# Float32r products with stacked split parts for the samples' A, the decay gates, and the diagonal and last level of a GLA head

## The chip, the cores and the metric

One core of one Trainium2 chip runs the whole program. The metric is the device time of one execution in microseconds; the time of a version is the median of its runs.

## The reference

One layer of a hybrid decoder runs on 256 prompt tokens and on 8 samples of 8 tokens (320 tokens, model width 2048), in float32:

```python
h = rmsnorm(x);  proj = h @ w_in          # q, k, v, gates of both branches
log_a = log_sigmoid(gal @ gla_alpha_up + gla_alpha_bias) / 16      # gal: 16 wide
# GLA head, chunk of L tokens (128 prompt, 8 sample); b = cumsum(log_a)
a_mat[t, s] = sum_d q[t, d] k[s, d] exp(b[t, d] - b[s, d])   for s <= t
o = a_mat @ v + (q * exp(b)) @ S
# mLSTM head: the same with one decay per token, D, and a normaliser column
num = (q k^T * D) @ v + w_inter * (q @ C);  den = the same on a column of ones
x = x + (sig(g_A) * (y_m @ W_A) + sig(g_B) * (y_g @ W_B)) @ W_out
x = x + ConvFFN(rmsnorm(x))
```

There are 4 heads of each branch (GLA: 128 keys, 256 values; mLSTM: 256 and 256). The outputs are y and the new states.

## The kernel before, in words

Activations lie transposed: features on the partitions, 320 tokens in the free dimension. Every large product is done in float32r on split operands: `weights` (L63) loads 512 KB, ScalarE rounds it (L69, `wh`), VectorE takes the rest (L70, `wl`), and `mm3` (L73) multiplies high by high (L74), high by low (L75) and low by high (L76), each a 128x128 weight against 320 columns. Weights pass through rings of 3 (`wh`, `wl`) and 4 (`raw`) buffers; products land in 4 PSUM banks named `big`, everything else in 4 named `mx`.

The work in order: norm and first projections (to 48 us), the gate block L310 to L408, then for each of 4 heads the projection of v, `gla_head` (L551), the projections of q, k and v, and `mlstm_head` (L654), to about 480 us; then gates, branch and output products and the ConvFFN, to the end. The program is given to a scheduler that runs a timeline simulation and writes one fixed order for each engine's queue. Engines keep that order, so an instruction that waits holds back everything behind it on its engine. In the head stage the scheduler mixes the small products of a head with the large products of the next projections on TensorE.

What the change touches:

- **Decay gates.** L297 loads the 16x512 matrix `alup` by a POOL DMA to partitions 64 to 79. L330 evacuates `galT`. L346 makes four float32 products of 16 rows, 320 columns each.
- **`values`** (L449), run once per head of each branch: v is transposed, ScalarE and VectorE write `vH` and `vL` (L463, L464), `vt` is a float32 copy for the samples (L468), `vs` holds v of 32 sample tokens four times over, the lower two quarters reduced to the low part (L470, L471). POOL writes the columns of ones and zeros on each call (L461, L462, L466).
- **`gla_head`**: the matrix A^T (`AT`) is filled by parts. L563 makes its diagonal: three float32 products k^T q, of 128, 128 and 64 tokens, from which only the diagonal is taken (L564, L565). L566 runs over eight levels hh = 128, 64, ..., 1: VectorE forms the decay exponents (L577, L578), ScalarE the exponential (L579), POOL multiplies k and q by it (L580, L581), and TensorE multiplies in float32 (L589 for each half of the prompt, L598 for the samples where hh <= 4), and VectorE copies the level's blocks by a mask (L592, L600).
- **Samples' A times v.** `inter` (L535) sums q times the old state into `pi`; then POOL (L609, in GLA) or VectorE (L708, in mLSTM) spreads the 64x64 sample A over `asp`, and one float32 product of 64 rows adds it to `pi` (L610, L710). `numerators` (L474) does the prompt's part on split operands (L485).
- **State updates** L645 and L732 multiply `vs` by masked keys in float32r.
- L408 and L669 pass the mLSTM gate rows through DRAM and back, spread over the partitions (`bc`), on POOL's DMA queue; L680 is the first reader.

A float32 matrix product shows in the trace as two records for each call, a float32r product or a transpose as one.

Of the kernel before, what the change touches and what calls it, by code (L numbers as in the profile page):

```python
# [17 lines left out]
P = 128  # L18
# [4 lines left out]
S = 8  # L23
# [20 lines left out]
def step_kernel(ctx: ExitStack, tc: tile.TileContext, a: dict):  # L44
# [52 lines left out]
    ones = cp.tile([P, P], F32, name="ones")  # L97
    nc.vector.memset(ones, 1.0)
    epsc = cp.tile([P, 1], F32, name="epsc")
    nc.gpsimd.memset(epsc, EPS)  # L100
# [132 lines left out]
    with tc.tile_pool(name="mc", bufs=1, reuse_waits="tile") as mc, \  # L233
# [61 lines left out]

        alup = mg.tile([P, 512], F32, name="alup")
        nc.gpsimd.dma_start(alup[64:80], a["gla_alpha_up"][0])  # L297
        mp9 = mc.tile([4, 9], F32, name="mp9")
# [30 lines left out]
        galT = mg.tile([P, N], F32, name="galT")  # L329
        nc.vector.tensor_tensor(galT[64:80], pg[64:80, :N], rstd_bc[64:80], op=ALU.mult)  # L330
        fr = w320("fr")[32:36]
        nc.vector.tensor_tensor(fr, pg[32:36, :N], rstd_bc[32:36], op=ALU.mult)
# [11 lines left out]
        for h in range(H):  # L344
            pz = mx("mx10")
            nc.tensor.matmul(pz[:, :N], alup[64:80, h * P:(h + 1) * P], galT[64:80], start=True, stop=True)  # L346
            xb = w320("xb")
            nc.vector.tensor_scalar(xb, pz[:, :N], abias[:, h:h + 1], None, op0=ALU.add)
            gb.append(gb5[:, h])
            nc.vector.scalar_tensor_tensor(gb[h], xb, -1.0, xb, op0=ALU.mult, op1=ALU.min)  # L350
            gx.append(xb)
# [60 lines left out]

        asp = mc.tile([64, P], F32, name="asp")
        nc.gpsimd.memset(asp, 0.0)

# [33 lines left out]
        def values(v):  # L449

            pb = mx("mx8")
            for m in range(2):
                vr, vr4 = quads("vr")
                nc.gpsimd.tensor_copy(vr4, tok4(v[:, m, T:]))
                for g in range(2):
                    nc.tensor.transpose(pb[:, g * 256 + m * P:g * 256 + (m + 1) * P], vr[:, g * P:(g + 1) * P], ident)
            pa = natural(v)
            pav = pa.rearrange("p (j e) -> p j e", j=2)
            vH = wk.tile([P, 2, 264], F32R, tag="vH", name="vH", bufs=1)[:, :, 0:258]
            vL = wk.tile([P, 2, 264], F32R, tag="vL", name="vL", bufs=1)[:, :, 0:258]  # L460
            nc.gpsimd.memset(vH[:, :, 256:258].bitcast(F32), 1.0)  # L461
            nc.gpsimd.memset(vL[:, :, 256:258].bitcast(F32), 0.0)  # L462
            nc.scalar.activation(vH[:, :, 0:256], pav, AF.Copy)  # L463
            nc.vector.tensor_tensor(vL[:, :, 0:256], pav, vH[:, :, 0:256].bitcast(F32), op=ALU.subtract)  # L464
            vt = wk.tile([64, 260], F32, tag="vt", name="vt", bufs=1)
            nc.gpsimd.memset(vt[:, 256:257], 1.0)  # L466
            for g in range(2):
                nc.scalar.copy(vt[32 * g:32 * g + 32, 0:256], pb[32 * g:32 * g + 32, g * 256:(g + 1) * 256])  # L468
            vs = wk.tile([P, 512], F32R, tag="vs", name="vs", bufs=1)
            nc.scalar.activation(vs, pb, AF.Copy)  # L470
            nc.vector.tensor_tensor(vs[64:128], pb[64:128], vs[64:128].bitcast(F32), op=ALU.subtract)  # L471
            return (vH, vL, vt), vs

        def numerators(name, A, vn, w):  # L474

            vH, vL, vt = vn
            AH = wk.tile([P, 384], F32R, tag="AH", name="AH", bufs=1)
# [73 lines left out]
        def gla_head(h, q, k, v):  # L551

            st0 = wk.tile([P, B, DV + 4], F32, tag="state", name="S0", bufs=3)[:, :, 0:DV]
            nc.sync.dma_start(st0, a["state_gla_S"][0, :, h].rearrange("b d e -> d b e"))
            vn, vs = values(v)
            b = gb[h]
            AT = wk.tile([P, 512], F32, tag="AT", name="AT")
            nc.gpsimd.memset(AT, 0.0)
            ATp = AT.rearrange("p (j c) -> p j c", j=2)[:, :, 0:P]
            ATs = AT[0:64, 384:448]  # L560
            pd = mx("mx11")
            for j, (t0, tn) in enumerate(TOK):
                nc.tensor.matmul(pd[:tn, t0:t0 + tn], k[:, t0:t0 + tn], q[:, t0:t0 + tn], start=True, stop=True)  # L563
            nc.vector.copy_predicated(ATp, dg8, pd[:, 0:256].rearrange("p (j c) -> p j c", j=2))  # L564
            nc.vector.copy_predicated(ATs, dg8[0:64, 0, 0:64], pd[0:64, 256:320])  # L565
            for hh in (128, 64, 32, 16, 8, 4, 2, 1):  # L566
                w = N if hh <= 4 else T
# [40 lines left out]
            pi = inter(qe, lambda b, d: st0[:, b], 256)  # L608
            nc.gpsimd.tensor_copy(srows(asp), ATs.rearrange("p (g q t) -> p g q t", g=2, q=4))  # L609
            nc.tensor.matmul(pi[:, 0:256], asp, vn[2][:, 0:256], start=False, stop=True)  # L610
            normed(list(numerators("mx13", AT, vn, 256)) + [pi], ghw[:, 2 * h:2 * h + 2], 8 + 2 * h)
# [25 lines left out]
            for b0 in range(0, B, 4):  # L637
# [4 lines left out]
                for i in range(0, 4, 2):  # L642
                    pS = mx("mx16")
                    for ii in range(2):
                        nc.tensor.matmul(pS[:, ii * 256:(ii + 1) * 256], kmv[:, i + ii], vs[:, 64 * b0:64 * b0 + 256],  # L645
                                         start=True, stop=True)
                    for ii in range(2):
                        bb = b0 + i + ii
                        nc.vector.scalar_tensor_tensor(st0[:, bb], st0[:, bb], ebe[:, bb:bb + 1],
                                                       pS[:, ii * 256:(ii + 1) * 256], op0=ALU.mult, op1=ALU.add)  # L650
# [3 lines left out]
        def mlstm_head(h, q, k, v):  # L654
            c0t = []
            for half in range(2):
# [3 lines left out]
                c0t.append(t)  # L660
            vn, vs = values(v)
            pa = natural(k)
# [22 lines left out]
            for half in range(2):  # L685
                nc.gpsimd.tensor_copy(c0t[half][:, :, :, DH], n0h[:, :, 4 * half:4 * half + 4].rearrange("p d b -> p b d"))
            n1 = nT[:, :, 4:36].rearrange("p d (b h) -> p d b h", h=H)[:, :, :, h]
# [12 lines left out]
            ks = stacked(pk, 512)  # L700
            pi = inter(qi, lambda b, d: c0t[b // 4][:, b % 4, d, 0:DH + 1], DH + 1)
            pS = mx("mx18")
            for d in range(2):
# [3 lines left out]
            nc.vector.tensor_tensor(D[:, 0:384], D[:, 0:384], pS[:, 0:384], op=ALU.mult)  # L707
            nc.vector.tensor_tensor(srows(asp), D[0:64, 384:448].rearrange("p (g q t) -> p g q t", g=2, q=4),  # L708
                                    pS[0:64, 384:448].rearrange("p (g q t) -> p g q t", g=2, q=4), op=ALU.mult)
            nc.tensor.matmul(pi[:, 0:DH + 1], asp, vn[2][:, 0:DH + 1], start=False, stop=True)  # L710
            normed(list(numerators("mx21", D, vn, DH + 2)) + [pi], mhw[:, 2 * h:2 * h + 2], 2 * h,
# [10 lines left out]
            for b0 in range(0, B, 2):  # L722
# [5 lines left out]
                for i in range(2):  # L728
                    bb = b0 + i
                    pC = mx("mx24")  # L730
                    for d in range(2):
                        nc.tensor.matmul(pC[:, d * 256:(d + 1) * 256], kmv[:, i, d * P:(d + 1) * P],  # L732
                                         vs[:, 256 * (b0 // 4):256 * (b0 // 4) + 256], start=True, stop=True)
                    cf = c0t[bb // 4][:, bb % 4, :, 0:DH]
# [246 lines left out]
```

## Time and profile before

| | us |
|---|---|
| median of 3 runs (1931.51 to 1933.71) | 1931.62 |
| the profiled execution, its own time | 1933.11 |
| its span, first to last instruction | 1931.4 |
| TensorE busy in the span | 1914.0 |
| VectorE / ScalarE / GpSimd busy | 1069.6 / 763.1 / 325.6 |

The span is 1.7 us below the execution's own time, and that execution is 1.5 us above the median. Busy time of TensorE counts a matmul until its result has left the array, so neighbours overlap in it; what one costs is read from the distance of the starts.

### The profile page before, as it was taken

The numbers are of one execution on the slowest core, as the hardware profiler recorded it, in microseconds if no ns is written. First come the engines' busy times: TensorE is split into PE (matmuls) and PEld (weight loads), VectorE is DVE, ScalarE is ACT, GpSimd is POOL, SyncE is SP. The second block draws the span as 40 slices with busy tenths as digits, with TensorE's granted clock in tenths as the row PEclk, the third lists the DMA queues.
The fourth block names the chain that finished last, engine by engine and source line by source line (L and its number), as shares of the span: only waits on it lengthen the run. The fifth ranks groups of instructions, "written<-read, shape, count | busy, mean of one in ns | idle before, by whom it ended". The sixth has DMA issues, their size and how long they took to land.

```text
span 1931.4 us, 32475 instructions
## 1 busy us (share of the span) xinstructions
PE 1914.0 (99%) x13143; PEld 1886.9 (98%) x13143; DVE 1069.6 (55%) x1627; ACT 763.1 (40%) x1063; POOL 325.6 (17%) x622
## 2 busy tenths in 40 slices
PE   9999999999999999999999999999999999999997
PEld 8989999999999999999999999999999999999997
DVE  5757676767544444445555545545554554555455
ACT  5434343454433333333344333433433343333335
POOL 4222232333000000012121101201110120111014
PEclk9999999999999999999999999999999999999999
DMA  8646666666655555556444444444444444444442
GB/s 238 197 117 191 196 186 202 189 194 191 193 148 148 152 153 146 149 156 202 146 149 152 153 147 149 153 151 144 152 153 148 148 153 152 144 152 153 149 148 95
DMA packets 300128, 310.96 MB, mean 161 GB/s; under 512 B 15237, under 2 KB 291995, under 8 KB 299978
## 3 DMA queue, kind: packets, MB, share of 16 engines
q1 hardware_dynamic: 287849, 283.53, 48.7%
q0 software_dynamic: 7232, 23.84, 3.6%
q8 instruction: 103, 1.69, 0.4%
q10 hardware_dynamic: 4896, 1.52, 0.3%
q14 instruction: 48, 0.39, 0.1%
HBM read 286.37 MB, written 22.47 MB: 160 GB/s over the span
## 4 chain that ended last, share of the span: by engine, by line


## 5 line engine op out<-in xcount | busy, mean ns | idle before, releaser
L70 DVE TENSOR_TENSOR wl<-raw,wh 128x1024 fp32r<-128x1024 f32 x504 | 629.2, 1248 | 623.9 <-ACT wh L69 623.0
L69 ACT ACTIVATE wh<-raw 128x1024 fp32r<-128x1024 f32 x504 | 534.3, 1060 | 900.0 <-PE big L75 766.2
L74 PE MATMUL big<-hH,wh 128*128 128x320 f32 x2832 | 880.6, 311 | 0.0
L75 PE MATMUL big<-hL,wh 128*128 128x320 f32 x2832 | 880.3, 311 | 0.0
L76 PE MATMUL big<-hH,wl 128*128 128x320 f32 x2832 | 879.6, 311 | 0.0
L76 PEld LDWEIGHTS big<-hH,wl 128*128 128x128 f32 x2832 | 533.1, 188 | 3.2 <-issue 2.6
L74 PEld LDWEIGHTS big<-hH,wh 128*128 128x128 f32 x2832 | 533.5, 188 | 1.9 <-issue 1.2
L75 PEld LDWEIGHTS big<-hL,wh 128*128 128x128 f32 x2832 | 533.4, 188 | 0.9 <-issue 0.4
L75 PE MATMUL big<-aL,wh 128*128 128x320 f32 x704 | 217.9, 310 | 0.0
L76 PE MATMUL big<-aH,wl 128*128 128x320 f32 x704 | 217.6, 309 | 0.0
L74 PE MATMUL big<-aH,wh 128*128 128x320 f32 x704 | 215.8, 309 | 0.0
L76 PEld LDWEIGHTS big<-aH,wl 128*128 128x128 f32 x704 | 132.4, 188 | 0.0
L75 PEld LDWEIGHTS big<-aL,wh 128*128 128x128 f32 x704 | 132.4, 188 | 0.0
L74 PEld LDWEIGHTS big<-aH,wh 128*128 128x128 f32 x704 | 131.8, 188 | 0.0
L876 POOL COPY conv<-u 128x2 f32<-128x2 f32 x44 | 8.2, 186 | 527.5 <-DVE u L873 527.5
L75 PE MATMUL big<-mL,wh 128*128 128x320 f32 x256 | 78.8, 309 | 0.0
L74 PE MATMUL big<-mH,wh 128*128 128x320 f32 x256 | 78.7, 309 | 0.0
L76 PE MATMUL big<-mH,wl 128*128 128x320 f32 x256 | 78.7, 309 | 0.0
L807 POOL TENSOR_TENSOR g<-g 128x320 f32<-128x320 f32 x16 | 14.7, 919 | 369.6 <-DVE g L803 369.6
L914 DVE TENSOR_TENSOR x<-big,x 128x320 f32<-128x320 f32 x96 | 46.6, 488 | 44.4 <-PE big L76 44.3
L888 POOL TENSOR_TENSOR g<-g,uc 128x256 f32<-128x256 f32 x44 | 32.5, 739 | 211.9 <-DVE g L887 211.9
L75 PE MATMUL big<-yL,wh 128*128 128x320 f32 x192 | 59.2, 308 | 0.0
(360 smaller groups left out, 1751.0 us busy)
## 6 DMA issues: line engine op xcount, KB each, us to landing
raw<-in_w_in SPq DMA_DIRECT2D x176, 512.0 KB, 3.7
raw<-in_ffn_w_up SPq DMA_DIRECT2D x88, 512.0 KB, 3.5
raw<-in_ffn_w_gate SPq DMA_DIRECT2D x88, 512.0 KB, 3.5
raw<-in_ffn_w_down SPq DMA_DIRECT2D x88, 512.0 KB, 3.5
raw<-in_w_out SPq DMA_DIRECT2D x32, 512.0 KB, 3.5
C<-in_state_mlstm_C SPq DMA_DIRECT2D x32, 256.0 KB, 5.5
o_C_s<-C POOLq DMA_DIRECT2D x32, 256.0 KB, 4.0
raw<-in_w_branch_a SPq DMA_DIRECT2D x16, 512.0 KB, 3.4
```

The source lines that it names most:

```text
L69: nc.scalar.activation(hi, raw, AF.Copy)
L70: nc.vector.tensor_tensor(lo, raw, hi.bitcast(F32), op=ALU.subtract)
L74: nc.tensor.matmul(out, wh, xh, start=first, stop=False)
L75: nc.tensor.matmul(out, wh, xl, start=False, stop=False)
L76: nc.tensor.matmul(out, wl, xh, start=False, stop=last)
L807: nc.gpsimd.tensor_tensor(sg[m], sg[m], acc[m], op=ALU.add)
L876: nc.gpsimd.tensor_copy(conv1[:, 0:2, c], u[:, T:T + 2])
L888: nc.gpsimd.tensor_tensor(g[:, 0:T], g[:, 0:T], gel[m][:, 0:T], op=ALU.mult)
L914: nc.vector.tensor_tensor(x2[k], pt[:, :N], x2[k], op=ALU.add)
```

## The change

Three kinds of small float32 products become float32r products on split operands, with the high and low parts stacked on the partitions so that one product sums several of the partial products.

1. Gates: `alup` and `galS` become zeroed 128-row tiles with a 16-row part in three strips (rows 0, 32 and 64), so that high*high, high*low and low*high come out of one 128-row float32r product per head.
2. Diagonal and last level (hh = 1): the sums over features are formed as products `pr` of q and k (POOL) with the decay of a pair of neighbours, split, and summed by a 128x128 matrix of ones: two float32r products of 480 columns. The loop ends at hh = 2.
3. Samples' A: `sample_values` copies the 32x32 block of each group by quadrants to `asp`, high parts by ScalarE and low parts by VectorE, and multiplies by `vs` in two float32r products of 128 rows.

`vH`, `vL` and `vs` become fixed tiles whose constant columns are written once; `vt` goes; the mLSTM normaliser column is doubled (258 columns for 257).

```diff
+    onesr = cp.tile([P, P], F32R, name="onesr")
+    nc.vector.memset(onesr.bitcast(F32), 1.0)
...
-        alup = mg.tile([P, 512], F32, name="alup")
-        nc.gpsimd.dma_start(alup[64:80], a["gla_alpha_up"][0])
+        alup = mc.tile([P, 512], F32R, name="alup")
+        galS = mc.tile([P, N], F32R, name="galS")
+        alur = mg.tile([P, 512], F32, name="alur")
+        nc.gpsimd.memset(alup.bitcast(F32), 0.0)
+        nc.gpsimd.memset(galS.bitcast(F32), 0.0)
+        for r in (0, 32, 64):
+            nc.gpsimd.dma_start(alur[r:r + 16], a["gla_alpha_up"][0])
+        for r in (0, 32, 64):
+            nc.scalar.activation(alup[r:r + 16], alur[r:r + 16], AF.Copy)
+        nc.vector.tensor_tensor(alup[64:80], alur[64:80], alup[64:80].bitcast(F32), op=ALU.subtract)
...
+        for r in (0, 64):
+            nc.scalar.activation(galS[r:r + 16], galT[64:80], AF.Copy)
+        nc.vector.tensor_tensor(galS[32:48], galT[64:80], galS[64:80].bitcast(F32), op=ALU.subtract)
...
-            nc.tensor.matmul(pz[:, :N], alup[64:80, h * P:(h + 1) * P], galT[64:80], start=True, stop=True)
+            nc.tensor.matmul(pz[:, :N], alup[:, h * P:(h + 1) * P], galS, start=True, stop=True)
...
-        asp = mc.tile([64, P], F32, name="asp")
+        asp = mc.tile([P, 2, P], F32R, name="asp")
...
-            for g in range(2):
-                nc.scalar.copy(vt[32 * g:32 * g + 32, 0:256], pb[32 * g:32 * g + 32, g * 256:(g + 1) * 256])
...
+        def sample_values(pi, A, w):
+            for g in range(2):
+                Ag = A[32 * g:32 * g + 32, 32 * g:32 * g + 32].rearrange("p (q t) -> p q t", t=S)
+                def quad(r):
+                    return asp[32 * r:32 * r + 32, g].rearrange("p (q y) -> p q y", q=4)[:, :, 8 * g:8 * g + 8]
+                for r in (g, g + 2):
+                    nc.scalar.activation(quad(r), Ag, AF.Copy)
+                for r in (1 - g, 3 - g):
+                    nc.vector.tensor_tensor(quad(r), Ag, quad(g).bitcast(F32), op=ALU.subtract)
+            for g in range(2):
+                nc.tensor.matmul(pi[:, 0:w], asp[:, g], vs[:, g, 0:w], start=False, stop=(g == 1))
...
+            pr = wk.tile([P, 480], F32, tag="pr", name="pr", bufs=1)
+            b2, q2, k2 = (t.rearrange("p (i x) -> p i x", x=2) for t in (b, q, k))
+            d1, p1 = w320("d1")[:, 0:160], pr[:, 320:480]
+            nc.vector.tensor_tensor(d1, b2[:, :, 1], b2[:, :, 0], op=ALU.subtract)
+            nc.scalar.activation(d1, d1, AF.Exp, scale=1.0 / 16)
+            nc.gpsimd.tensor_tensor(pr[:, 0:N], q, k, op=ALU.mult)
+            nc.gpsimd.tensor_tensor(p1, q2[:, :, 1], k2[:, :, 0], op=ALU.mult)
+            nc.gpsimd.tensor_tensor(p1, p1, d1, op=ALU.mult)
+            prH, prL = (wk.tile([P, 480], F32R, tag=t, name=t, bufs=1) for t in ("prH", "prL"))
+            nc.scalar.activation(prH, pr, AF.Copy)
+            nc.vector.tensor_tensor(prL, pr, prH.bitcast(F32), op=ALU.subtract)
             pd = mx("mx11")
-            for j, (t0, tn) in enumerate(TOK):
-                nc.tensor.matmul(pd[:tn, t0:t0 + tn], k[:, t0:t0 + tn], q[:, t0:t0 + tn], start=True, stop=True)
+            nc.tensor.matmul(pd[:, 0:480], onesr, prH, start=True, stop=False)
+            nc.tensor.matmul(pd[:, 0:480], onesr, prL, start=False, stop=True)
...
+            nc.vector.copy_predicated(ATp.rearrange("p j (b x) -> p j b x", x=2)[:, :, :, 1], lvl[1],
+                                      pd[:, 320:448].rearrange("p (j b) -> p j b", j=2))
+            nc.vector.copy_predicated(ATs.rearrange("p (b x) -> p b x", x=2)[:, :, 1], lvl[1][0:64, 0, 0:32],
+                                      pd[0:64, 448:480])
-            for hh in (128, 64, 32, 16, 8, 4, 2, 1):
+            for hh in (128, 64, 32, 16, 8, 4, 2):
...
-            nc.gpsimd.tensor_copy(srows(asp), ATs.rearrange("p (g q t) -> p g q t", g=2, q=4))
-            nc.tensor.matmul(pi[:, 0:256], asp, vn[2][:, 0:256], start=False, stop=True)
+            sample_values(pi, ATs, 256)
...
-            nc.tensor.matmul(pi[:, 0:DH + 1], asp, vn[2][:, 0:DH + 1], start=False, stop=True)
+            sample_values(pi, D[0:64, 384:448], DH + 2)
```

## Rows read from the trace of the kernel before

**Rows 1.** The page's first part: busy time, share, instructions of each engine.
```profile
PE 1914.0 (99%) x13143; PEld 1886.9 (98%) x13143; DVE 1069.6 (55%) x1627; ACT 763.1 (40%) x1063; POOL 325.6 (17%) x622
```
**Rows 2.** Windows: length, busy us (count) of PE, PEld, DVE, ACT, POOL; clock, DMA share, GB/s.
```profile
200.00:300.00 100.00, 100.00 (x729) 95.44 (x728) 72.06 (x150) 40.57 (x78) 31.53 (x54) 1.00 0.66 201
...
500.00:600.00 100.00, 100.00 (x684) 100.00 (x683) 48.22 (x59) 38.43 (x49) 1.75 (x2) 1.00 0.54 156
```
**Rows 3.** Waits of TensorE by line: total us, times, longest.
```profile
PE mx L589 <- DVE AT L592: 4.2, 1, 4.2
```
**Rows 4.** Timeline of VectorE: start, us, instruction, idle before it and releaser.
```profile
103.92 0.29 DVE L680 TENSOR_TENSOR qi<-q,bc 128x128 f32<-128x128 f32 x1 [5.26 <-DMA bc<-rows]
```
**Rows 5.** Windows of time around that wait, columns as in rows 2.
```profile
101.70:106.20 4.50, 0.30 (x3) 0.03 (x1) 2.28 (x9) 0.10 (x1) 0.00 (x0) 0.97 0.31 115
106.20:112.70 6.50, 6.50 (x26) 6.50 (x27) 4.86 (x14) 3.52 (x6) 4.26 (x7) 0.50 0.56 163
```
**Rows 6.** Timeline of TensorE, head 0: the samples' A and products of 256 columns.
```profile
127.10 0.28 PE L485 MATMUL mx<-vH,AH 128*128 128x256 f32 x1
...
127.57 0.32 PE L74 MATMUL big<-hH,wh 128*128 128x320 f32 x1
...
130.09 0.31 PE L75 MATMUL big<-hL,wh 128*128 128x320 f32 x1
130.33 0.70 PE L610 MATMUL mxi<-vt,asp 64*128 64x256 f32 x2
...
131.21 0.31 PE L74 MATMUL big<-hH,wh 128*128 128x320 f32 x1
```
**Rows 7.** Timeline of TensorE, head 1: the diagonal's products.
```profile
199.44 0.31 PE L76 MATMUL big<-hH,wl 128*128 128x320 f32 x1
199.58 0.86 PE L563 MATMUL mx<-gq,gk 128*128 128x128 f32 x6
...
200.63 0.31 PE L75 MATMUL big<-hL,wh 128*128 128x320 f32 x1
```
**Rows 8.** Timeline of TensorE, head 0: a level's products for prompt and samples.
```profile
98.51 0.31 PE L74 MATMUL big<-hH,wh 128*128 128x320 f32 x1
98.66 0.33 PE L589 MATMUL mx<-lv_z 128*128 128x64 f32 x2
...
99.03 0.31 PE L76 MATMUL big<-hH,wl 128*128 128x320 f32 x1
...
126.23 0.31 PE L74 MATMUL big<-hH,wh 128*128 128x320 f32 x1
126.47 0.30 PE L598 MATMUL mx<-lv_z 128*64 128x32 f32 x2
...
126.95 0.31 PE L76 MATMUL big<-hH,wl 128*128 128x320 f32 x1
```
**Rows 9.** Timeline of TensorE, gate block: the decay gates' products.
```profile
63.60 0.31 PE L76 MATMUL big<-hH,wl 128*128 128x320 f32 x1
...
65.90 0.31 PE L75 MATMUL big<-hL,wh 128*128 128x320 f32 x1
...
67.80 0.31 PE L76 MATMUL big<-hH,wl 128*128 128x320 f32 x1
68.04 0.80 PE L346 MATMUL mx<-galT,alup 16*128 16x320 f32 x2
...
69.02 0.31 PE L75 MATMUL big<-hL,wh 128*128 128x320 f32 x1
```
**Rows 10.** Groups by line and shape: busy us, mean ns, idle before and releasers.
```profile
L463 ACT ACTIVATE vH<-mx 128x512 fp32r<-128x512 f32 x8 | 4.7, 591 | 1.1 <-PE mx L446 1.1
...
L464 DVE TENSOR_TENSOR vL<-mx,vH 128x512 fp32r<-128x512 f32 x8 | 5.5, 688 | 0.2
```
**Rows 11.** Timeline of POOL, head 0: the two multiplications of a level.
```profile
107.90 1.21 POOL L580 TENSOR_TENSOR lv_z<-gk,lv_d 128x160 f32<-128x160 f32 x1 [0.38 <-ACT lv_d L579]
109.07 0.61 POOL L581 TENSOR_TENSOR lv_z<-gq,lv_d 128x160 f32<-128x160 f32 x1
```

More of the change, by code (lines that the diff above doesn't have):

```diff
@@ L410, in step_kernel @@
         nT = mc.tile([P, 2, 36], F32, name="nT")
-        asp = mc.tile([64, P], F32, name="asp")
-        nc.gpsimd.memset(asp, 0.0)
+        asp = mc.tile([P, 2, P], F32R, name="asp")
+        nc.gpsimd.memset(asp.bitcast(F32), 0.0)
+        vH, vL, vs = (mc.tile([P, 2, 264], F32R, name=t)[:, :, 0:258] for t in ("vH", "vL", "vs"))
+        for t, one in ((vH, 1.0), (vL, 0.0), (vs[0:64], 1.0), (vs[64:128], 0.0)):
+            nc.gpsimd.memset(t[:, :, 256:258].bitcast(F32), one)
         def proj2(tag, c0, scale):
@@ L458, in values @@
             pav = pa.rearrange("p (j e) -> p j e", j=2)
[L459 to L462, printed above, removed]
             nc.scalar.activation(vH[:, :, 0:256], pav, AF.Copy)
             nc.vector.tensor_tensor(vL[:, :, 0:256], pav, vH[:, :, 0:256].bitcast(F32), op=ALU.subtract)
-            vt = wk.tile([64, 260], F32, tag="vt", name="vt", bufs=1)
-            nc.gpsimd.memset(vt[:, 256:257], 1.0)
-            for g in range(2):
-                nc.scalar.copy(vt[32 * g:32 * g + 32, 0:256], pb[32 * g:32 * g + 32, g * 256:(g + 1) * 256])
[L469 to L472, printed above, removed]
+            pbv = pb.rearrange("p (g e) -> p g e", g=2)
+            nc.scalar.activation(vs[:, :, 0:256], pbv, AF.Copy)
+            nc.vector.tensor_tensor(vs[64:128, :, 0:256], pbv[64:128], vs[64:128, :, 0:256].bitcast(F32), op=ALU.subtract)
+            return vH, vL
+        def sample_values(pi, A, w):
+            for g in range(2):
+                Ag = A[32 * g:32 * g + 32, 32 * g:32 * g + 32].rearrange("p (q t) -> p q t", t=S)
[7 more added lines that the diff above has]
+                nc.tensor.matmul(pi[:, 0:w], asp[:, g], vs[:, g, 0:w], start=False, stop=(g == 1))
         def numerators(name, A, vn, w):
-            vH, vL, vt = vn
+            vH, vL = vn
             AH = wk.tile([P, 384], F32R, tag="AH", name="AH", bufs=1)
@@ L554, in gla_head @@
             nc.sync.dma_start(st0, a["state_gla_S"][0, :, h].rearrange("b d e -> d b e"))
-            vn, vs = values(v)
+            vn = values(v)
             b = gb[h]
@@ L644, in gla_head @@
                     for ii in range(2):
-                        nc.tensor.matmul(pS[:, ii * 256:(ii + 1) * 256], kmv[:, i + ii], vs[:, 64 * b0:64 * b0 + 256],
+                        nc.tensor.matmul(pS[:, ii * 256:(ii + 1) * 256], kmv[:, i + ii], vs[:, b0 // 4, 0:256],
                                          start=True, stop=True)
@@ L660, in mlstm_head @@
                 c0t.append(t)
-            vn, vs = values(v)
+            vn = values(v)
             pa = natural(k)
@@ L685, in mlstm_head @@
             for half in range(2):
-                nc.gpsimd.tensor_copy(c0t[half][:, :, :, DH], n0h[:, :, 4 * half:4 * half + 4].rearrange("p d b -> p b d"))
+                for c in (DH, DH + 1):
+                    nc.gpsimd.tensor_copy(c0t[half][:, :, :, c], n0h[:, :, 4 * half:4 * half + 4].rearrange("p d b -> p b d"))
             n1 = nT[:, :, 4:36].rearrange("p d (b h) -> p d b h", h=H)[:, :, :, h]
@@ L700, in mlstm_head @@
             ks = stacked(pk, 512)
-            pi = inter(qi, lambda b, d: c0t[b // 4][:, b % 4, d, 0:DH + 1], DH + 1)
+            pi = inter(qi, lambda b, d: c0t[b // 4][:, b % 4, d, 0:DH + 2], DH + 2)
             pS = mx("mx18")
@@ L707, in mlstm_head @@
             nc.vector.tensor_tensor(D[:, 0:384], D[:, 0:384], pS[:, 0:384], op=ALU.mult)
-            nc.vector.tensor_tensor(srows(asp), D[0:64, 384:448].rearrange("p (g q t) -> p g q t", g=2, q=4),
-                                    pS[0:64, 384:448].rearrange("p (g q t) -> p g q t", g=2, q=4), op=ALU.mult)
-            nc.tensor.matmul(pi[:, 0:DH + 1], asp, vn[2][:, 0:DH + 1], start=False, stop=True)
+            nc.vector.tensor_tensor(D[0:64, 384:448], D[0:64, 384:448], pS[0:64, 384:448], op=ALU.mult)
+            sample_values(pi, D[0:64, 384:448], DH + 2)
             normed(list(numerators("mx21", D, vn, DH + 2)) + [pi], mhw[:, 2 * h:2 * h + 2], 2 * h,
@@ L732, in mlstm_head @@
                         nc.tensor.matmul(pC[:, d * 256:(d + 1) * 256], kmv[:, i, d * P:(d + 1) * P],
-                                         vs[:, 256 * (b0 // 4):256 * (b0 // 4) + 256], start=True, stop=True)
+                                         vs[:, b0 // 4, 0:256], start=True, stop=True)
                     cf = c0t[bb // 4][:, bb % 4, :, 0:DH]
```

## The prediction

> **What bounds the kernel now.** I read the totals first: TensorE is busy for 1914.0 of 1931.4 us, VectorE for 55%, ScalarE for 40%, POOL for 17% [rows 1]. Busy time alone proves little, since neighbouring matmuls overlap in it, so I looked at stretches. Between 500 and 600 us TensorE does nothing but large products, and 684 start in 100 us: one every 0.146 us, without a gap [rows 2]. In the head stage, 200 to 300 us, TensorE is busy the whole time too, with VectorE at 72%, ScalarE at 41% and POOL at 32% [rows 2]. The list of waits says the same from the other side: behind the kernel's first microseconds TensorE waits once, for 4.2 us, for a masked copy of VectorE in head 0 [rows 3]. VectorE is late there because it stood 5.26 us waiting for the gate rows that come back from DRAM [rows 4]. The wait is paid twice: in the 6.5 us behind it the granted clock is 0.50, the 1.2 GHz level [rows 5]; 26 matmuls start there, worth 26 x 0.146 = 3.8 us at the other level, so about 2.7 us are lost. Wait and clock together cost 4.2 + 2.7 = 6.9 us.
>
> So the time is the sum of what TensorE is given to do, and a product is worth the stretch of TensorE's queue that it takes. I price each by the start of the large product ahead of it and the start of the second large product behind it, less two large products (0.292 us). The second one is needed because the first one behind a small product is itself late.
>
> **Samples' A (4 GLA and 4 mLSTM heads).** From 130.09 to 131.21 is 1.12 us, less 0.292: the float32 product of 64 rows takes 0.83 us [rows 6]. In its place come two float32r products of 256 or 258 columns. Four such products take from 127.10 to 127.57, so 0.118 each [rows 6], 0.235 for two. Gain 0.59 a head, **4.7 us** for eight. The operation and the width are the ones in the row, so I give this no wide bounds (4.4 to 4.9).
>
> **Diagonal.** The three float32 products take 1.19 - 0.292 = 0.90 us [rows 7]. The two products of 480 columns have no row. The nearest are the large ones of 320 columns at 0.146 [rows 2]; in proportion to the columns 480 take 0.219. As bounds I take 0.146 (columns cost nothing more) and 0.292 (twice the row). With 0.219 the gain is 0.90 - 0.44 = 0.46 a head, **1.8 us** for four; by the bounds 1.3 to 2.4.
>
> **Last level (hh = 1).** For each half of the prompt a float32 product takes 0.52 - 0.292 = 0.23 us [rows 8]: two in each of four heads, **1.8 us**. The samples' one takes 0.72 - 0.292 = 0.43 us when it stands alone [rows 8]. Where it stands beside another product of its own shape it must cost less, because the cost of its narrow shape is then shared; I take the 0.23 of its neighbour in the same rows, so **0.9 us** for four, and bounds of 0.4 and 1.7.
>
> **Decay gates.** From 63.60 to 65.90 three of the four float32 products and the two small transposes of L306 take 2.30 - 0.292 = 2.01 us; the fourth takes 1.22 - 0.292 = 0.93 [rows 9]. Together 2.94. Four float32r products of 320 columns are four large products, 0.58. The transposes stay and had been partly covered; alone they may cost anything from 0 to the 0.43 of a small product of another shape [rows 8], and I take 0.43 as it is the nearest in shape. Gain 2.94 - 0.58 - 0.43 = **1.9 us**, at most 2.4.
>
> The widening of `inter` from 257 to 258 columns, and the fixed tiles for v, I cost at nothing.
>
> **The sum** is 4.7 + 1.8 + 1.8 + 0.9 + 1.9 = 11.1 us, by the bounds 9.8 to 13.2. The profiled execution took 1933.11 us, its span 1931.4; its like would take 1922.0, with a span of 1920.3. That execution lies 1.5 us above the median of 1931.62, so the median should come to **1920.5 us**.
>
> **What is added beside TensorE, and its cover.** In a GLA head ScalarE loses the exponential of one level and two copies of v, and gains a shorter exponential, a rounding of 480 columns (0.59 by the 512-column row) and four small quadrant copies; VectorE loses two subtractions and three masked copies and gains one subtraction, one of 480 columns (0.69 by the 512-column row) [rows 10], two masked copies and four small ones. Either is at most about 1 us a head and branch, 8 us in 400; VectorE has 28 us idle in each 100 and ScalarE 59 [rows 2]. If that cover were gone, the splits of the weights would come late and TensorE would wait for `wl`; no such wait is in the list now [rows 3]. POOL trades two multiplications and the copy to `asp` for three multiplications, and loses the writing of constant columns in each head, which had waited for readers of the last head. Its two further loads of `alup` and two clearings stand early in its queue, ahead of masks that nobody needs before the heads; POOL is busy 32% even in the heads [rows 2]. The gates' chain becomes longer by two ScalarE copies and a subtraction; `alup` is now cleared only when the first stage's memory is free, and ScalarE's three copies of it wait for that, with roundings of weights queued behind them. The three buffers of `wh` cover this: each holds 24 products, 3.5 us of TensorE. The ScalarE copies to `asp` wait for the last masked copy of A, as POOL did; behind them stand roundings again, with the same cover.
>
> **The rivals.** (1) *The wait of head 0 goes.* Its cause is a DMA landing that the fixed order did not allow for [rows 4], and the order is written anew. If VectorE's first reader of the gate rows comes later in its queue, TensorE gets back up to 6.9 us: 1913.6. Against it: the path through DRAM is not changed, and the scheduler's view of it is not either.
>
> (2) *A second wait of that kind appears, or that one doubles.* TensorE reaches the spot sooner, since the gates and the diagonal have become 2 us shorter, while the landing does not. One more such wait with its slow clock costs 6.9 us: 1927.4. For it: one landing of that sort was missed already; against it: the three other heads have none [rows 3].
>
> (3) *Slower: the diagonal's chain stops TensorE in every head.* Before, L563 needed only q and k. Now three POOL multiplications, a rounding and a subtraction stand ahead of `pd`. A POOL multiplication of 160 columns took 0.61 us, and 1.21 in the row above it [rows 11]; the chain is four such widths, 2.4 to 4.8 us, plus 0.59 and 0.69 [rows 10], so 3.7 to 6.1 us. If the order puts `pd` where L563 stood, everything behind it on TensorE waits. It decides against the change from 11.1 / 4 = 2.8 us a head. By the upper price, four heads lose 24 us: 1931.6 - 11.1 + 24.4 = 1944.9. Against it: the scheduler places a product when its inputs are due, and it has large products of the next projection to put ahead.
>
> The Trainium skill's page "SBUF — State Buffer", section "Who interferes with whom", says that a VectorE instruction with two SBUF inputs and a GpSimd instruction that reads SBUF block one another for a whole instruction. The trace agrees in so far as the same multiplication takes 0.61 or 1.21 us [rows 11]. By the rule the upper price of (3) is the usual one, since the weight split L70 is of that kind.
>
> (4) *The new products are not faster.* If a product of 480 columns took a float32 product's time, only the diagonal's 1.8 us would be lost: still 1922. The other float32r shapes stand in the rows.
>
> **How the numbers follow.** The forecast, TensorE's cut with the wait of head 0 about as it is, has 0.56: 1920.5, by the bounds and 2 us of that wait either way 1916.5 to 1924. Rival (1) has 0.17, (2) 0.17, (3) 0.06; 0.04 is for a mixture that cancels the gain. The range 1912.5 to 1929 takes in (1) and (2) and leaves out (3). About 0.2%, 3.9 us, is what a measurement of this kernel can tell from no change. Faster by more than that are the forecast, (1) and the better part of (2), 0.84; within it the rest of (2), the mixture and the mild end of (3), 0.11; slower 0.05.
>
> **What would show it.** Right: no float32 records on the gates, the diagonal and the samples' A; 480-column products 0.2 to 0.23 us apart; 0.118 for the new products of 256 columns, with no late product behind them; one wait of TensorE of about 4 us, in head 0; span about 1920. Wrong: waits of TensorE for `pd`, for `wl` or for `asp` in heads 1 to 3, a second stretch of clock 0.50, or 480-column products far from 0.22 us.

## The result and the profile after

The changed kernel took 1919.19 us (median of 4 runs, 1918.81 to 1919.85), the one before on the same chip 1932.16 (4 runs, 1931.51 to 1933.71): a ratio of 0.9931 [0.9917, 0.9946], 13.0 us faster. In a later job it was 1917.97 against 1932.66, 0.9923 [0.991, 0.9937]. The forecast was 1920.5. The profiled execution took 1919.33, its span is 1917.6.

The page's first part, and windows of time with the columns of [rows 2] and [rows 5] (the first and third are new):

```profile
PE 1900.5 (99%) x13099; PEld 1880.2 (98%) x13099; DVE 1076.6 (56%) x1658; ACT 770.0 (40%) x1088; POOL 336.6 (18%) x614
```
```profile
9.50:16.30 6.80, 6.56 (x23) 5.74 (x24) 5.17 (x8) 3.49 (x8) 1.23 (x4) 0.50 1.09 305
105.10:108.50 3.40, 3.40 (x15) 3.40 (x14) 2.26 (x11) 1.37 (x2) 1.60 (x4) 0.50 0.46 155
200.00:300.00 100.00, 100.00 (x745) 96.22 (x745) 72.51 (x158) 41.31 (x81) 32.60 (x48) 1.00 0.67 206
```

TensorE has lost 13.5 us of busy time [rows 1], and starts 745 products instead of 729 in the same 100 us of the head stage [rows 2]. VectorE, ScalarE and POOL are each 7 to 11 us busier in the whole span, and about 1 us or less in these 100. Up to the last large product the views give half clock (0.50) in two places: for 3.4 us in head 0, where there were 6.5 [rows 5], and for 6.8 us at the start. The second is not new: the section on the start shows that the kernel before runs its first products at half rate as well, but not for as long.

The waits of TensorE, to be read against [rows 3]:

```profile
PE mx L631 <- POOL lv_z L623: 2.0, 1, 2.0
PE big L74 <- ACT wh L69: 2.0, 1, 2.0
```

The one wait behind the first microseconds is 2.0 us instead of 4.2, and what it waits for is another thing: a multiplication of POOL, not a masked copy of VectorE.

The timeline of TensorE, for the gates (first group), the diagonal in head 0, a level product of the samples in head 0, and the samples' A in head 1; a product is priced as in the prediction, by the large products around it:

```profile
65.48 0.31 PE L76 MATMUL big<-hH,wl 128*128 128x320 f32 x1
65.72 0.30 PE L317 MATMUL mx<-ident,n0r 32*128 32x32 f32 x2
65.95 0.71 PE L360 MATMUL mx<-galS,alup 128*128 128x320 f32 x3
...
66.64 0.30 PE L75 MATMUL big<-hL,wh 128*128 128x320 f32 x1
...
98.47 0.38 PE L600 MATMUL mx<-prH,onesr 128*128 128x480 f32 x1
98.69 0.31 PE L76 MATMUL big<-hH,wl 128*128 128x320 f32 x1
...
121.06 0.31 PE L76 MATMUL big<-hH,wl 128*128 128x320 f32 x1
121.29 0.30 PE L640 MATMUL mx<-lv_z 128*64 128x32 f32 x2
...
121.78 0.31 PE L75 MATMUL big<-hL,wh 128*128 128x320 f32 x1
...
219.52 0.28 PE L498 MATMUL mxi<-vs,asp 128*128 128x256 f32 x1
219.63 0.31 PE L75 MATMUL big<-hL,wh 128*128 128x320 f32 x1
219.78 0.30 PE L76 MATMUL big<-hH,wl 128*128 128x320 f32 x1
```

Three gate products with L317 take 66.64 - 65.48 - 0.29 = 0.87 us, where [rows 9] gave 2.01. A product of 480 columns takes 98.69 - 98.47 = 0.22. One of 256 takes 219.63 - 219.52 = 0.11, and nothing behind it is late. The samples' level product still costs 121.78 - 121.06 - 0.29 = 0.43 alone, and the two that stand side by side in heads 1 to 3 take 0.55, priced in the same way.

**Where the time went.** Every kernel here starts the same 12,144 large products, in the same order but for at most 15 of them between the 163rd and the 433rd, so the start of the n-th of them in two traces says how much has been gained by then. Gain against the kernel before, in us (worked out from the starts of L74, L75 and L76; the 41st stands in the first microseconds, the 461st behind the gates, the 1121st, 1661st and 2201st behind GLA heads 1, 2 and 3, the 2421st behind the last mLSTM head):

| kernel | 41st | 461st | 1121st | 1661st | 2201st | 2421st | last |
|---|---|---|---|---|---|---|---|
| after | -1.89 | 0.04 | 8.22 | 10.76 | 13.30 | 13.83 | 13.84 |
| gates alone | -0.51 | 1.41 | 5.32 | 5.30 | 5.30 | 5.30 | 5.30 |
| diagonal and last level alone | -0.86 | -0.86 | 6.77 | 8.10 | 9.45 | 9.39 | 9.40 |
| samples' A alone | -0.34 | -0.34 | 1.50 | 2.69 | 3.84 | 4.40 | 4.40 |

In the changed kernel the gates give 1.93 (from the 41st to the 461st), and a GLA head with an mLSTM head 2.54 (from the 1121st to the 1661st, and again to the 2201st). Work cut is so 1.93 + 4 x 2.54 = 12.1 us. From the 41st on 13.84 + 1.89 = 15.73 are gained; the 3.6 left over fall between the 461st and the 1121st, where head 0's wait lies. The start takes 1.9 back. Behind the heads nothing moves.

### The profile page after: what moved, and what is told of

It is laid out like the page before. It is cut to its first block, busy times and chain, and to the rows that moved or that the text cites. A ratio compares the mean times of both kernels' runs of the same rounds, so it can differ in the third digit from the quotient of the medians.

```text
span 1917.6 us, 32433 instructions
## 1 busy us (share of the span) xinstructions
PE 1900.5 (99%) x13099; PEld 1880.2 (98%) x13099; DVE 1076.6 (56%) x1658; ACT 770.0 (40%) x1088; POOL 336.6 (18%) x614
## 4 chain that ended last, share of the span: by engine, by line
## 5 line engine op out<-in xcount | busy, mean ns | idle before, releaser
L74 PE MATMUL big<-hH,wh 128*128 128x320 f32 x2832 | 880.2, 311 | 2.0 <-ACT wh L69 2.0
L75 PE MATMUL big<-hL,wh 128*128 128x320 f32 x2832 | 879.7, 311 | 0.0
L76 PE MATMUL big<-hH,wl 128*128 128x320 f32 x2832 | 878.9, 310 | 0.0
L74 PEld LDWEIGHTS big<-hH,wh 128*128 128x128 f32 x2832 | 533.4, 188 | 2.5 <-ACT wh L69 2.1
L75 PEld LDWEIGHTS big<-hL,wh 128*128 128x128 f32 x2832 | 533.3, 188 | 1.8 <-issue 1.2
L76 PEld LDWEIGHTS big<-hH,wl 128*128 128x128 f32 x2832 | 533.2, 188 | 1.0 <-issue 0.4
L75 PE MATMUL big<-aL,wh 128*128 128x320 f32 x704 | 217.9, 310 | 0.0
L76 PE MATMUL big<-aH,wl 128*128 128x320 f32 x704 | 217.6, 309 | 0.0
L74 PE MATMUL big<-aH,wh 128*128 128x320 f32 x704 | 215.8, 309 | 0.0
L76 PEld LDWEIGHTS big<-aH,wl 128*128 128x128 f32 x704 | 132.4, 188 | 0.0
L75 PEld LDWEIGHTS big<-aL,wh 128*128 128x128 f32 x704 | 132.4, 188 | 0.0
L74 PEld LDWEIGHTS big<-aH,wh 128*128 128x128 f32 x704 | 131.8, 188 | 0.0
L75 PE MATMUL big<-mL,wh 128*128 128x320 f32 x256 | 78.8, 309 | 0.0
L74 PE MATMUL big<-mH,wh 128*128 128x320 f32 x256 | 78.7, 309 | 0.0
L76 PE MATMUL big<-mH,wl 128*128 128x320 f32 x256 | 78.7, 309 | 0.0
L75 PE MATMUL big<-yL,wh 128*128 128x320 f32 x192 | 59.2, 308 | 0.0
```

Of the source, the lines that this page charges most:

```text
L74: nc.tensor.matmul(out, wh, xh, start=first, stop=False)
L75: nc.tensor.matmul(out, wh, xl, start=False, stop=False)
L76: nc.tensor.matmul(out, wl, xh, start=False, stop=last)
```

## The experiments

**The three parts one by one.** Each is the kernel before with one part of the change (gates; diagonal with last level; samples' A with the fixed tiles for v).

```diff
 # e1_gates
-            nc.tensor.matmul(pz[:, :N], alup[64:80, h * P:(h + 1) * P], galT[64:80], start=True, stop=True)
+            nc.tensor.matmul(pz[:, :N], alup[:, h * P:(h + 1) * P], galS, start=True, stop=True)
 # e2_diag
+            nc.tensor.matmul(pd[:, 0:480], onesr, prH, start=True, stop=False)
+            nc.tensor.matmul(pd[:, 0:480], onesr, prL, start=False, stop=True)
-            for hh in (128, 64, 32, 16, 8, 4, 2, 1):
+            for hh in (128, 64, 32, 16, 8, 4, 2):
 # e3_asp
-            nc.tensor.matmul(pi[:, 0:256], asp, vn[2][:, 0:256], start=False, stop=True)
+            sample_values(pi, ATs, 256)
```

> The kernel before with the decay gates alone changed. Theory (TensorE's queue is the time): the four products of the gates and the two transposes of L306 take about 1.0 us of TensorE's queue instead of 2.94, so 1.9 us less behind the gate block; the wait of head 0 stays near 4 us. If the three loads of the small matrix on POOL's queue are what makes the first weights land 1 us later in the changed kernel, the start of this kernel is late by 1 to 1.9 us too, and the span is 1931 to 1932, as before. If that late start is chance, the span is 1929.5. Rival (the gates are covered by other work): span 1931.4 whatever the start.

> The kernel before with the diagonal and the last level alone changed. Theory: 0.46 us a head for the diagonal, 0.46 for the prompt's last level, 0.43 for the samples' last level, 1.35 us a head, 5.4 us in all, and one load of the gates' matrix, so the start is as before: span 1926 with the wait of head 0 as before (4.2 us and 2.7 us of slow clock), 1922 to 1924 if the new order makes that wait shorter as in the changed kernel. Rival (the sums' chain on POOL, ScalarE and VectorE stops TensorE): a wait of 2 us or more for the first product of 480 columns in each head, span 1930 or above.

> The kernel before with the samples' A alone changed (and the fixed tiles for v). Theory: 0.59 us for each of eight heads, 4.7 us: span 1926.7, start as before, wait of head 0 as before or within 2 us of it. Rival (the copies to asp on ScalarE hold back the roundings of the weights): waits of TensorE for wh or wl in the heads, span 1929 or above.

Measured: the gates alone 1928.21 us, 0.9981 [0.9972, 0.999]; the diagonal alone 1923.68, 0.9959 [0.9945, 0.9973]; the samples' A alone 1928.55, 0.998 [0.9971, 0.9989]. By the table, behind the start and outside head 0's wait: gates 1.92; diagonal and last level 1.33 and 1.35 a head; samples' A 4.40 + 0.34 = 4.74 (its wait in head 0 stayed, at 4.0 us), or 0.59 for each of eight heads. So the work cut is 1.9 + 5.4 + 4.7 = 12.0 us, and the work of the parts adds up to the whole.

What was missed is head 0's wait. The waits of TensorE with the gates alone:

```profile
PE mx L601 <- POOL lv_z L593: 1.7, 1, 1.7
```

with the samples' A alone:

```profile
PE mx L601 <- DVE AT L604: 4.0, 1, 4.0
```

and a window of head 0 with the diagonal alone:

```profile
100.00:110.00 10.00, 7.62 (x52) 7.13 (x53) 9.90 (x25) 3.83 (x7) 8.80 (x13) 1.00 0.42 107
```

Only the second is the old wait. With the gates alone, which cut no work in head 0, 3.9 us came back there (from 1.41 to 5.32); with the diagonal alone TensorE still waits in head 0 (7.62 of 10 us busy), but its clock stays at 1.00, and 5.0 us came back (from -0.86 to 6.77, less two GLA heads at 1.34). With the gates alone it was the new order of the instructions that did it, not less work. What each part alone gets back in head 0 does not add up either: the whole change got back 3.6.

**How head 0's wait came to be shorter.** In the kernel before, VectorE reached its first reader of the gate rows at 103.92 - 5.26 = 98.66 and stood for 5.26 us with level copies behind it [rows 4]. The timelines of the changed kernel, POOL and then VectorE:

```profile
95.10 0.52 POOL L422 DMA_DIRECT2D rows<-R  x1
...
101.88 0.62 POOL L710 DMA_DIRECT2D bc<-rows  x1 [2.82 <-DMA rows<-R]
...
103.19 0.45 POOL L623 TENSOR_TENSOR lv_z<-gq,lv_d 128x128 f32<-128x128 f32 x1
```
```profile
106.24 0.29 DVE L721 TENSOR_TENSOR qi<-q,bc 128x128 f32<-128x128 f32 x1 [3.31 <-DMA bc<-rows]
```

The rows land later than before, 106.24 against 103.92, but the reader stands later in VectorE's queue by more, at 102.93 against 98.66, with the two subtractions of a level and a weight split now just ahead of it. In its place POOL stands still: the load of `bc` waits 2.82 us for the store of the rows, and two level multiplications are queued behind it. L631 waits for those.

The way through DRAM takes about as long as before: from the issue of the store to the first reader 106.24 - 95.10 = 11.1 us, and before 103.92 - 92.26 = 11.7. But its slow half has changed. The time from issue to landing of the store of the rows and the four loads of `bc` together, before and after:

```profile
DMA to landing us min/median/max: 2.9/4.4/8.5
DMA to landing us min/median/max: 4.0/4.2/6.5
```

Before, the store took 2.9 us and head 0's load 8.5, and VectorE stood for the load. Now the store takes 6.5 and no load more than 4.3; VectorE still stands for the load, 3.31 us, but what TensorE waits for stands behind POOL's wait for the store. In the new order the two small stores of `o_m` (L402, L403) stand just ahead of the store of the rows on POOL's queue; before, they stood behind it and ahead of the load. Whether they are what made the transfer behind them slow is not shown: with the diagonal alone they stand ahead of the load, and no load takes more than 4.3.

The 2.0 us wait and 15 matmuls at half clock (3.4 - 15 x 0.146 = 1.2 us) cost 3.2 together, against the 6.9 of before: 3.7 less, beside 3.6 in the table.

To test that the path through DRAM is the whole of what is left, head 0's `bc` was loaded from an input that needs no store (the gate rows of mLSTM head 0 are then other data):

```diff
-            nc.gpsimd.dma_start(bc, rows_d[h:h + 1].broadcast_to([P, 456]))
+            src = a["norm_mix_w"][0:1, 0:456] if h == 0 else rows_d[h:h + 1]
+            nc.gpsimd.dma_start(bc, src.broadcast_to([P, 456]))
```

> The changed kernel, with the gate rows of mLSTM head 0 read from an input of the same size that is there from the start, so that VectorE has nothing to wait for; the outputs of mLSTM head 0 are made from other data. Theory (the landing of the rows is the only cause of the wait in head 0): no wait of VectorE for the rows, no wait of TensorE in head 0, no slow clock there; 2.0 us of wait and about 1.5 us of slow clock come back, span 1914. Rival (TensorE waits in head 0 for the levels' chain anyway): a wait of about 2 us stays, span within 1 us of 1917.6.

Measured 1914.64 us, 0.991 [0.9893, 0.9926]. From the 461st product to the end this kernel gains 17.08 us, the changed one 13.80: 3.3 more. Its one wait of TensorE behind the start, and a window of head 0:

```profile
PE mx L631 <- ACT AT L627: 0.5, 1, 0.5
```
```profile
100.00:110.00 10.00, 9.46 (x68) 9.02 (x67) 9.39 (x27) 3.91 (x7) 5.41 (x8) 1.00 0.48 145
```

With the rows early, 0.5 us of waiting stays in head 0 and no half clock. So what is left of the wait comes with the way through DRAM. How much of it is the store's landing, and how much the place of the load and its reader in their queues, this run does not separate: the order is written anew here too, and the load is issued at 55.3 us, far ahead of this stretch.

**Two ways to get the rows sooner.** The first leaves DRAM out: one DMA spreads a row of `R` from its partition in SBUF to all 128.

```diff
-        nc.gpsimd.dma_start(rows_d, R1)
-            nc.gpsimd.dma_start(bc, rows_d[h:h + 1].broadcast_to([P, 456]))
+            nc.gpsimd.dma_start(bc, R1[h:h + 1].unsqueeze(1).broadcast_to([1, P, 456]))
```

> The changed kernel with the gate rows spread over the partitions by one DMA from SBUF, without the way through DRAM; the arithmetic is the same. Theory: the rows land about 5 us earlier, since the first DMA and POOL's wait for it go, the waits in head 0 go, span 1914. Rival (a read of one partition by 128 descriptors is slow, or the order moves): the rows land as late or later, and the wait stays or grows; span 1917 to 1922.

Measured 1934.0 us, 1.0005 [0.9995, 1.0014]: the whole gain of the change is gone. The list of DMA issues (queue, count, KB each, median us to landing), first of this kernel, then of the changed one, and the largest wait of TensorE and of VectorE with the SBUF source:

```profile
bc<-R POOLq DMA_DIRECT2D x4, 228.0 KB, 10.4
```
```profile
bc<-rows POOLq DMA_DIRECT2D x4, 228.0 KB, 4.1
```
```profile
PE mxi L571 <- DVE vs L480: 7.6, 3, 2.6
```
```profile
DVE dec L722 <- DMA bc<-R: 17.1, 3, 5.7
```

The load takes 10.4 us instead of 4.1, nearly as long as the whole way through DRAM in head 0 (11.1), and now VectorE stands for it in every head (4.8 us in head 0, 5.7 at most in the others), and TensorE behind it, each time with a stretch of half clock after it. This is what rival (2) looks like when it comes true.

The second makes head 0's rows on TensorE: a float32 product of a row of ones with row 0 of `R`, and a copy by ScalarE.

```diff
+        nc.tensor.matmul(pr0[:, 0:456], ones[0:1], R1[0:1], start=True, stop=True)
+        nc.scalar.copy(bc0, pr0[:, 0:456])
```

> The changed kernel with the gate rows of head 0 spread over the partitions by one float32 product of a row of ones (456 columns) and a copy by ScalarE, in place of the way through DRAM; heads 1 to 3 as before, and the arithmetic the same. Theory: the product costs some 0.95 us of TensorE's queue, the waits of VectorE and TensorE in head 0 and the slow clock there go (3.3 us, as with the early rows): 2.3 us less than the changed kernel behind the start, span 1913.5 to 1915.5 by how late it starts. Rival (the order moves, or the product holds TensorE while the rows are made): a new wait of TensorE of 2 us or more near 95 us, span 1916 or above.

Measured 1915.22 us, 0.9911 [0.9898, 0.9925]; behind the 461st product 16.92 us are gained, 3.1 more than by the change alone. The product's row and the wait that stays:

```profile
94.54 1.01 PE L424 MATMUL mxr<-R,ones 1*128 1x456 f32 x2
```
```profile
PE mx L635 <- POOL lv_z L627: 0.7, 1, 0.7
```

The product takes about a microsecond of TensorE's queue; the wait of head 0 falls from 2.0 to 0.7 us, and its half clock is gone.

**The samples' level products as 128-column weights.** If the 0.43 us of such a product is the change of its shape (64 weight columns among 128), padding its weights to 128 columns must bring it to the prompt's 0.23.

```diff
-                    nc.tensor.matmul(pl[0:64, 128:160], zs, zs.rearrange
+                    nc.tensor.matmul(pl[:, 128:160], z[:, T:384], zs.rearrange
```

> The changed kernel with the samples' two remaining level products taken over 128 columns of weights (64 of them zero) in place of 64, so that they have the shape of their neighbours. Theory (what makes them cost 0.43 us alone is the change of shape): a pair of records takes 0.23 us of TensorE's queue as the prompt's do, two adjacent pairs 0.44 instead of 0.54; 0.4 us less in head 0, 0.1 in each other head, 0.7 us in all. Rival (a small product costs 0.43 whatever its shape, or the wider weights cost more): no change.

Measured 1917.54 us in one execution; a gain of this size is read from the trace, not from the total. The timeline of TensorE, a level product of the samples and the run of narrow state products (L576) in head 0:

```profile
114.94 0.31 PE L76 MATMUL big<-hH,wl 128*128 128x320 f32 x1
115.09 0.33 PE L635 MATMUL mx<-zw 128*128 128x64 f32 x2
115.35 1.07 PE L576 MATMUL mxi<-S,qz 128*32 128x256 f32 x16
116.35 0.43 PE L635 MATMUL mx<-zw 128*128 128x64 f32 x2
...
116.83 0.30 PE L75 MATMUL big<-hL,wh 128*128 128x320 f32 x1
...
119.96 0.31 PE L74 MATMUL big<-hH,wh 128*128 128x320 f32 x1
120.11 0.30 PE L644 MATMUL mx<-zw 128*128 128x32 f32 x2
...
120.48 0.31 PE L76 MATMUL big<-hH,wl 128*128 128x320 f32 x1
```

The same product, padded, takes 120.48 - 119.96 - 0.29 = 0.23: the other 0.2 us was the shape. Behind the 461st product the kernel gains 15.17, that is 1.4 more than the change. By the prices 0.4 of it are head 0's two lone products and 0.3 the pairs of heads 1 to 3 (0.45 each instead of 0.55). The other 0.7 comes from the order: here the 16 narrow products stand together, while in the changed kernel a level product stands between them:

```profile
115.78 0.31 PE L75 MATMUL big<-hL,wh 128*128 128x320 f32 x1
...
116.19 0.63 PE L572 MATMUL mxi<-S,qz 128*32 128x256 f32 x6
116.75 0.43 PE L631 MATMUL mx<-lv_z 128*128 128x64 f32 x2
117.11 1.05 PE L572 MATMUL mxi<-S,qz 128*32 128x256 f32 x10
...
118.35 0.30 PE L74 MATMUL big<-hH,wh 128*128 128x320 f32 x1
```

The same 18 products take 118.35 - 115.78 - 0.29 = 2.28 us there and 116.83 - 114.94 - 0.29 = 1.60 here. The run of narrow products that was left and entered again took 0.7 us longer.

**The start.** The changed kernel is 1.89 us late at the 41st product, and 0.92 at the first (9.57 against 8.65 us). The change adds two small loads to POOL's queue there, so one kernel loads `alup`'s source once and copies it three times, and the changed kernel ran twice more as it is.

```diff
-        for r in (0, 32, 64):
-            nc.gpsimd.dma_start(alur[r:r + 16], a["gla_alpha_up"][0])
+        nc.gpsimd.dma_start(alur[64:80], a["gla_alpha_up"][0])
```

> The changed kernel with one load of the gates' matrix; ScalarE copies it to the three strips. If the two further loads make the start late, the first large product starts near 8.7 us as in the kernel before, not 9.6, and the span falls by 1 to 1.9 us to 1916. If the late start is chance, or comes from the clearing of the ones on VectorE, the start stays late or goes either way.

> The changed kernel unaltered, one more profile. If the late start is a property of the program, the first large product starts at 9.6 us again, ScalarE waiting 1.5 us for the first weights, and the slow clock at the start ends 1 us later than in the kernel before. If it is chance, the start moves by some 0.5 us or more. Behind the start the two profiles should agree to 0.1 us.

> The changed kernel unaltered, timed beside the two below and profiled a third time. Expected: 1918 to 1920 us, behind the start the same trace as in the two profiles before, start late by 0 to 1.9 us if its lateness is chance.

Measured: one load 1917.69 us, late at the 41st product by 0.12; the unchanged kernel 1918.38 and 1917.97 (the second a median of 5), late by 0.83 and 1.71. From the 461st product on they gain 13.7, 13.7 and 13.0, the change's first profile 13.8. The 0.7 that the third is short lie in head 0, where its wait is 2.4 us: what is read from one trace there holds to about that much. ScalarE's timeline, its first rounding of weights and what it waited for, in the changed kernel's first profile and its second:

```profile
8.46 1.06 ACT L69 ACTIVATE wh<-raw 128x1024 fp32r<-128x1024 f32 x1 [1.51 <-DMA raw<-in_w_in]
```
```profile
7.68 1.06 ACT L69 ACTIVATE wh<-raw 128x1024 fp32r<-128x1024 f32 x1 [1.17 <-DMA raw<-in_w_in]
```

So the landing of the first weights moves by 0.8 us between two executions of one program. That is one part of the lateness; the other is the clock. TensorE's timeline in the kernel before:

```profile
13.31 0.47 PE L74 MATMUL big<-hH,wh 128*128 128x320 f32 x1
13.57 0.40 PE L75 MATMUL big<-hL,wh 128*128 128x320 f32 x1
```

These stand 0.26 us apart, about as in head 0's half clock (0.27, from 105.54 to 105.81 us in the changed kernel), and those from 13.81 on 0.15. The windows of that kernel give 1.00 for this stretch, but the first stretch of clock that its trace holds starts at 13.75; the products show that it ran at half rate until then. In the changed kernel half clock lasts until 16.34 us, in its second execution until 15.40. There the first product is only 0.14 us late and the 41st 0.83, so most of that is the clock. The kernels with three loads lie between 0.01 and 1.89 late, those with one (the kernel before among them) between 0.86 late and 0.04 early. The two sets overlap; whether the loads add to it stays open.

**What is best together.** Head 0's rows on TensorE, one load of `alup`'s source and the padded level products:

```diff
+        nc.tensor.matmul(pr0[:, 0:456], ones[0:1], R1[0:1], start=True, stop=True)
+        nc.gpsimd.dma_start(alur[64:80], a["gla_alpha_up"][0])
+                    nc.tensor.matmul(pl[:, 128:160], z[:, T:384], zs.rearrange
```

> The kernel of the run before with one load of the gates' matrix and the samples' level products 128 columns wide. Theory: 0.7 to 1.4 us less again behind the start, depending on where the order puts the level products among the narrow ones of inter: span 1912 to 1914.5, and the fastest of all runs with the right result. Rival (the order of head 0 is rewritten for the worse): span 1915 or above.

Measured 1914.26 us (4 runs, 1913.9 to 1914.65), 0.9906 [0.9892, 0.9919], beside 1917.97 for the changed kernel on the same chip: the fastest kernel here that computes all of the reference. It is not the sum of its parts: behind the 461st product it gains 17.23, only 0.3 more than the rows on TensorE alone. Its order was written anew too, and what that took back was not followed up.

## Why the prediction was right

**The total** was 1.3 us high in the median and 2.7 in the span (1920.3 against 1917.6); the profiled execution of before lay 1.5 us above its median, that of after 0.1. The 2.7 are misses that partly cancel: 0.9 us more work was cut than forecast and head 0's wait gave back 3.7, while the start of this execution took 1.9. So it is in part luck that the total came so near: with the start of the kernel before, the span would have been forecast 4.6 us too high.

**Samples' A**: forecast 4.7 us, measured 4.74. Operation and width stood in a row of before.

**Diagonal**: forecast 0.219 us for a product of 480 columns, by proportion from the large ones; measured 0.22. The cost is in the columns, and both bounds were too wide.

**Gates**: forecast 1.9, measured 1.93. Pricing the uncovered transposes at 0.43 was right: 0.87 for three products and the transposes is 3 x 0.146 + 0.43.

**Last level, samples**: this term was mis-sized. The prediction took 0.23 because a product beside one of its own shape must cost less. But of the three in each of heads 1 to 3, one had stood alone (0.43) and two together (0.54); now the two that stay stand together (0.55). So a lone one went, at its full 0.43, and in head 0 too the two that stay cost 0.43 each. Four heads give 1.7, the upper bound, and not 0.9; this is the 0.8 us of work that the sum missed.

**Head 0's wait "about as it is"** was the step that failed. Wait and clock cost 6.9 before and 3.2 after, a change of 3.7 where 2 either way was allowed. Rival (1) named the way (the first reader later in VectorE's queue), and half of it came; its reason against, that the path through DRAM is unchanged, held for the path as a whole (11.7 us before, 11.1 after) and not for its halves or the order around it. What it missed is the other end of that path: the load of `bc` waits on POOL as its reader waits on VectorE, and the multiplications behind it became the wait of TensorE.

**Rival (2)** did not come. Its sign, a second stretch of half clock, which the prediction had put down as a mark of being wrong, stands at the start, but it was a poor sign: the kernel before runs its first products at half rate too, until 13.75 us. The start as a whole, landing and clock, took 1.9 us in this execution and 0.83 in another of the same program.

**Rival (3)** did not come: TensorE waits for `pd` in no head. The groups of the diagonal's chain (mean ns of one):

```profile
L593 POOL TENSOR_TENSOR pr<-gq,gk 128x320 f32<-128x320 f32 x4 | 3.5, 886 | 16.2 <-DVE gk L131 16.2
L594 POOL TENSOR_TENSOR pr<-gq,gk 128x160 f32<-128x160 f32 x4 | 4.4, 1094 | 0.0
L595 POOL TENSOR_TENSOR pr<-pr,d 128x160 f32<-128x160 f32 x4 | 2.2, 540 | 0.1
L597 ACT ACTIVATE prH<-pr 128x480 fp32r<-128x480 f32 x4 | 2.4, 588 | 0.0
L598 DVE TENSOR_TENSOR prL<-pr,prH 128x480 fp32r<-128x480 f32 x4 | 2.6, 645 | 0.0
```

The sum is 3.75 us, the lower end of the 3.7 to 6.1, and the order put other work between, as the prediction said: in each head L593 starts 40 to 77 us ahead of L595. The mean of L594 hides two prices, 0.60 and 0.61 in two heads, 1.57 and 1.59 in the others. The timelines of POOL and of VectorE at one of the long ones:

```profile
231.62 1.57 POOL L594 TENSOR_TENSOR pr<-gq,gk 128x160 f32<-128x160 f32 x1
```
```profile
231.02 1.72 DVE L70 TENSOR_TENSOR wl<-raw,wh 128x1024 fp32r<-128x1024 f32 x1 [0.17 <-ACT wh L69]
```

The weight split beside it is longer too, 1.72 us against the 1.2 that it takes elsewhere. The Trainium skill's page "SBUF — State Buffer", section "Who interferes with whom", states that such a pair blocks one another; the two rows agree with it. Its upper price was paid by two of the twelve multiplications, not by most.

## What to carry to other kernels

Where one engine is full, price an edit by the stretch of its queue, with the products of another shape around it, and ask of a removed one whether it stood alone; such prices came out here within a few hundredths of a microsecond each. A wait that a fixed order caused is not a constant when the order is written anew: follow both ends of the transfer behind it, the engine that issues the load as well as the one that reads it, and list what is queued behind each. When the first weights land at another time from one execution to the next, compare two traces from a later product on.

## What the runs showed of the hardware

- A DMA that spreads one row of an SBUF partition over 128 partitions took 10.4 us for 228 KB; the same from DRAM 4.1 in the median, and up to 8.5 in head 0 of the kernel before.
- A float32 product with 64 weight columns among products with 128 cost 0.43 us alone, 0.23 with its weights padded; a level product in the midst of narrow state products cost 0.7 us more for the run than one beside it.
- In head 0 half clock (0.50, the 1.2 GHz level) followed waits of TensorE of 1.7 us (gates alone) and 2.0 us (changed kernel) for 3.4 us, and of 4.0 us (samples' A alone) and 4.2 us (before) for 6.8; it followed none where the longest was 0.5 (rows early), 0.7 (rows on TensorE) or 1.4 us (diagonal alone). The length of the wait alone does not settle it: at the start, waits of 1.4 to 2.0 us were followed by 6.8 us of half clock in the changed kernel, with the gates alone and with the diagonal alone, and one of 1.5 us by 3.4 us with the rows early.
- The first weights of one program landed up to 0.8 us apart in two executions, and the 41st product 1.1 us apart.
